# Doubled Strassen products: the order of wide and narrow matmuls in a decoder layer

## The chip, the cores and the metric

The kernel runs on one core of one Trainium2 chip. The engines are named as in the profile: PE (TensorE, matmuls), PEld (the weight loads of TensorE), DVE (VectorE), ACT (ScalarE), POOL (GpSimd) and SP (SyncE, which only issues DMAs here). The metric is the device time of one execution in microseconds; a kernel's time is the median of its runs.

## The reference, cut to what matters

One layer of a hybrid decoder on 512 tokens of width 2048, all in float32:

```python
h = rmsnorm(x, attn_norm_g[i])
proj = h @ w_in[i]                    # 2048 -> u, v, q, k, v_att (5 x 1024), g_a, g_b (2 x 2048)
y_a = chunked_spatial_gating(u, v_sgu, w_s[i], b_s[i])     # after gelu and a norm of v
y_b = stick_breaking_attention(q, k, v_att)                # 8 heads of 128, blocks of 128
merged = sigmoid(g_a) * (y_a @ w_up_a[i]) + sigmoid(g_b) * (y_b @ w_up_b[i])
x = x + merged @ w_o[i]
hid = rmsnorm(x, ffn_norm_g[i]) @ w_ffn_in[i]              # 2048 -> 2 x 5632
x = x + (silu(hid[..., :5632]) * hid[..., 5632:]) @ w_ffn_out[i]
x = x + sigmoid(rmsnorm(x, ple_norm_g[i]) @ w_ple_gate[i]) * (p[i] @ w_ple[i])
```

## The kernel before, in words

Everything is kept transposed: features on the 128 partitions, the 512 tokens along the free axis. A number is split into a high part, which the fast matmul format holds exactly, and a low rest (`split_into`, L266 and L267; for weights `split`, L331 on DVE and L334 on ACT). A product of two split numbers takes three matmuls: high by high, high by low, low by high (`mm3`, L271 to L273).

A matrix product is cut into *pairs*: a `Pair` computes one block of 256 output features for all 512 tokens. Its contraction over 2048 features has eight units of 256, of kind S (one step of Strassen: the 2 by 2 blocks need seven products of 128 x 128 weights with 256 tokens instead of eight) or P (plain). Two neighbouring units of one kind share a load of weights, so a pair of eight S units consists of four *calls* of `Pair.add`, each with two units (`n = 2`), that is with 7 x 2 products.

In two stages the pairs are *doubled* (`doubled=7` in the FFN input, 43 pairs; `doubled=5` in the input projection, 33 pairs). A doubled product owns a PSUM bank of 512 columns, and the three matmuls become two, both at L629 of the kernel before:

- a **wide** one ("both"): the high half of the weights against high and low half of the tokens side by side, 512 columns;
- a **narrow** one ("low"): the low half of the weights against the high half of the tokens, 256 columns, added to the first half of the bank.

With `doubled=5` the last two products of a call go through `mm3` with 256 columns and share the bank "y". Products 1 to 6 of `doubled=7` (0 to 5 in the code) take the six banks of the pool `psm`; the seventh takes one of the two banks of the pool `psa`, whose tiles the profile calls "small".

In a pair's first call the matmuls of a product clear its bank (`start`); in its last call (`stop`) each finished product is taken out of PSUM and mixed into the four output blocks by `mix_doubled` (ACT copies at L685, DVE additions at L688), step by step with `next(mix)`. Only when the last reader of a bank is done may the next pair write it.

The order on PE is that of the program, except where the tile framework's planner, which runs over the traced program with a model of the times, finds the next matmul not ready and takes a later one. On ACT and DVE the splits of weights and the mixing are chained in the order in which they were written (`in_turn`). Weights arrive ahead of their use: `prepare_early` at the head of a call and `prepare_late` after its third product advance the weights of the next two calls by a step (load on SP, an accumulating load on POOL at L338, sums on DVE at L350, splits); there are three slots of split weights (`whi`, `wlo`), and a call gives its slot back at its end. After the products listed in `TICKS` (the fourth and the seventh) `tick()` places pieces of other work: attention, gating, the forms of the next inputs.

In the kernel before, the two units of one doubled product follow each other as wide, narrow, narrow, wide.

Of the kernel before, what the change touches and what calls it, by code (L numbers as in the profile page):

```python
# [65 lines left out]
def hybrid_layer(  # L66
# [18 lines left out]
    nc = tc.nc  # L85
# [9 lines left out]
    def nm(s):  # L95
        return f"{s}_{next(names)}"
# [75 lines left out]

    def wide():
        return tmp.tile([P, 1024], F32, tag="out", name=nm("out"))
# [14 lines left out]
    def mark(instruction):  # L189
        newest[instruction.ins.engine] = instruction.ins.name  # L190
# [4 lines left out]
    def traced():  # L195
        return nc.cur_bb.bb.instructions

    def tick():

        clock[0] += 1  # L200
        last, units = traced()[-1], dict(newest)
        for f in list(builds)[:AHEAD]:
            if not f.there and f.ready() and fits([(wholes, 1024, "old"), (wholes, 1024, "low")]):
                f.fetch()
                break
        if builds and builds[0].ready() and builds[0].arrived() and fits(builds[0].sizes):
            builds.popleft().step()
        while waiting and waiting[0][0] <= clock[0]:
            heapq.heappop(waiting)[2]()
        for i in reversed(traced()):  # L210
            if i is last:
                break
            if i.engine in units:
                tc.add_manual_dep(
                    i, units[i.engine],
                    mybir.DependencyInfo(mybir.DependencyClass.NoSync,
                                         mybir.DependencyReason.DATA),
                    reason="in its place among the units")
# [50 lines left out]
    def mm3(ps, sh, sl, mh, ml, start, stop, halved=False):  # L269
        for s in (slice(0, 256), slice(256, T)) if halved else (slice(None),):  # L270
            nc.tensor.matmul(ps[:, s], sh, mh[:, s], start=start, stop=False)  # L271
        nc.tensor.matmul(ps, sh, ml, start=False, stop=False)  # L272
        return nc.tensor.matmul(ps, sl, mh, start=False, stop=stop)  # L273
# [109 lines left out]
    def prepare_early():  # L383

        if prepared:
            prepared[0].to(4)
        if len(prepared) > 1 and (slots or prepared[1].step > 1):
            prepared[1].to(3)

    def prepare_late():  # L390

        if len(prepared) > 1 and prepared[1].step > 1:
            prepared[1].to(4)
        for w in list(prepared)[2:]:
            w.to(1)
        ahead(8)

    def ahead(n):
        while planned and landings and len(prepared) < n:
            prepared.append(Weights(*planned.popleft()))  # L400
# [76 lines left out]
    def load(src, n=1024, how="old"):  # L477
        b = take(n, how)
        nc.sync.dma_start(out=b.f(0, 1024), in_=src)
        return b  # L480
# [91 lines left out]
    class Pair:  # L572
# [21 lines left out]
        def add(self, kind, ws, xs, prepare=True):  # L594
            n = len(ws)
            start = self.left[kind] == self.n[kind]
            self.left[kind] -= n
            stop = self.left[kind] == 0
            if prepare:
                prepare_early()  # L600
            if kind == "P":
                for u, ((wh, wl), (xh, xl)) in enumerate(zip(ws, xs)):
                    for ps, bs in zip(self.ends(), ((2, 3), (0, 1))):
                        for k, b in enumerate(bs):
                            first = start and u + k == 0

                            mark(mm3(ps, wh[:, b], wl[:, b], xh[k], xl[k],
                                     first and not self.both, stop and u == n - 1 and k == 1,
                                     first and self.both and b < 2))
                    if prepare and u == 0:  # L610
                        prepare_late()
                    tick()
                return

            if stop:
                o = self.home()
                self.o = wide() if o is None else o
                mix = (self.mix_doubled if self.doubled else self.mix)(self.o)
            for i, ((name, h), (w, x)) in enumerate(zip(HALVES, PRODUCTS)):
                for u, ((wh, wl), t) in enumerate(zip(ws, xs)):  # L620
                    first, last = start and u == 0, stop and u == n - 1
                    if i < self.doubled:
                        ps = self.at(i)
                        both = ps, wh[:, w], t[:, x].rearrange("p s c -> p (s c)")
                        low = ps[:, :256], wl[:, w], t[:, x, 0]

                        work = (low, both) if u else (both, low)
                        for k, (out, l, r) in enumerate(work):
                            m = nc.tensor.matmul(out, l, r, start=first and k == 0,  # L629
                                                 stop=last and k == 1)  # L630
                        mark(m)
                    else:


                        ps = self.at(name)[:, 256 * h : 256 * h + 256]
                        ends = not (self.both and name in "yz") and (h == 1 or name == "z")
                        mark(mm3(ps, wh[:, w], wl[:, w], t[:, x, 0], t[:, x, 1],
                                 first and h == 0, last and ends))
                if stop:
                    next(mix)  # L640
                if i == 2:
                    prepare_late()
                if i in TICKS[n]:
                    tick()

        def mix(self, o):

# [27 lines left out]
        def mix_doubled(self, o):  # L675
# [4 lines left out]
            c11, c12, c21, c22 = (b[:, i] for i in range(4))  # L680
            s5 = tmp.tile([P, 256], F32, tag="p5", name=nm("p5"), bufs=1)
            add, sub = ALU.add, ALU.subtract

            def copy(out, x, scale=1.0):
# [10 lines left out]
            yield  # L695
            copy(c22, p7[0])
            tt(c12, c12, c11, add)
            tt(c22, c22, p7[1], add)
            yield
            copy(s5, p5[0])  # L700
# [219 lines left out]
    def x_form(k):  # L920
        def steps(form):
            while len(x_raw) < min(k + 2, KU):
                load_x()
            form.blocks = (parts.take(2 * PLACE, "place"),)
            w = take(1024, "old")
            gained(w.f(), x_raw[k].f(), g_attn, k)
            norm1.add(x_raw[k])
            give(x_raw[k])
            yield
            yield from plain_first(form, w)  # L930
            return form.operand()

        return Form("S", steps, [], always)

    xs = [x_form(k) for k in range(KU)]
# [221 lines left out]
    order = []  # L1157
# [68 lines left out]
    for n, ((w, i), pr) in enumerate(zip(order, made())):  # L1226
# [24 lines left out]
        else:  # L1251
            d = tc.dram_tile([P, 1024], F32, name=nm("gsp"))
# [6 lines left out]
    part, merged = {}, {}  # L1259
# [30 lines left out]
    there = set()  # L1290
# [7 lines left out]
    for j in range(KU):  # L1298
# [9 lines left out]
        h = raw.popleft()  # L1308
# [37 lines left out]
    at = 0  # L1346
    for c, kinds in enumerate(PASSES):
        units, first = hs[at : at + len(kinds)], at
# [3 lines left out]
        for j in range(KU):  # L1352
# [6 lines left out]
            h = before.f()  # L1359
# [128 lines left out]
```

## Time and profile before

| what | value |
|---|---|
| time, three runs | 2701.99, 2707.65, 2710.27 us; median 2707.65 us |
| profiled execution | span 2701.9 us, which is the run of 2701.99 us to a tenth |
| PE busy | 2668.1 us (99%), 15875 matmuls |
| DVE busy | 2147.0 us (79%) |
| ACT busy | 1367.3 us (51%) |
| POOL busy | 459.0 us (17%) |
| DMA | 529.40 MB, mean 196 GB/s |

The windows of the trace that the text speaks of are, in us from the start: 0 to 87 the start of the input projection, 87 to 830 the rest of it with attention and gating beside it, 830 to 1204 the up and output projections, 1204 to 2047 the FFN input, 2047 to 2702 the FFN output and the last gate.

Matmuls are pipelined: the durations that the profile gives for them overlap, so a row of the timeline is read by its start, and the time that a matmul costs is the distance to the next start. Where neighbouring instructions of one line are merged, "x2" stands behind the row and the second start falls in between. PE's busy share hides short waits for the same reason.

### The profile page before, as it was taken

How to read it: one execution, taken by the hardware profiler on the slowest of the kernel's cores; microseconds unless marked ns; L12 is line 12 of the kernel's file. 1: busy time of each engine (PE TensorE's matmuls, PEld its weight loads, DVE VectorE, ACT ScalarE, POOL GpSimd, SP SyncE). 2: the span in 40 equal slices, each digit the busy share in tenths (PEclk: the TensorE clock that was granted, in tenths of full speed). 3: DMA queues.
4: the chain of work that ended last, by engine and by line, in shares of the span. 5: the costliest groups of instructions: out<-in, count | busy, mean ns of one | idle time of the engine just before them, and what ended most of it. 6: DMA issues, size and time to landing. Idle time of an engine off the chain costs nothing.

```text
span 2701.9 us, 43167 instructions
## 1 busy us (share of the span) xinstructions
PE 2668.1 (99%) x15875; PEld 2354.6 (87%) x15875; DVE 2147.0 (79%) x3621; ACT 1367.3 (51%) x2143; POOL 459.0 (17%) x543
## 2 busy tenths in 40 slices
PE   8999999999999999999999999999999999999999
PEld 6888888989998889988888888888888999988898
DVE  7687878787887566688988888888889667688776
ACT  7656565655554343374444444444445344453543
POOL 0232323232220000001111111111111111110110
PEclk9999999999999999999999999999999999999999
DMA  7677777777776467678888888888887668688784
GB/s 224 156 185 175 181 173 186 170 187 197 177 186 197 140 173 200 173 219 211 212 212 202 200 203 205 201 198 210 195 210 206 181 167 262 184 249 236 218 243 133
DMA packets 303268, 529.40 MB, mean 196 GB/s; under 512 B 25680, under 2 KB 162896, under 8 KB 303056
## 3 DMA queue, kind: packets, MB, share of 16 engines
q1 hardware_dynamic: 242304, 426.22, 49.9%
q0 software_dynamic: 60752, 100.43, 23.8%
q8 instruction: 124, 2.03, 0.3%
q14 instruction: 88, 0.72, 0.1%
HBM read 479.36 MB, written 47.19 MB: 195 GB/s over the span
## 4 chain that ended last, share of the span: by engine, by line
PE 88%; DVE 5%; DMA 2%; ACT 2%; issue 1%; POOL 1%; SPq 0%; DVEq 0%; ACTq 0%; POOLq 0%
PE ps L629 39%; PE ps L272 14%; PE ps L273 14%; PE ps L271 14%; PE small L629 4%; DVE wlo L331 2%; DVE out L688 1%; PE small L1084 1%; PE small L959 1%; ACT whi L334 1%; DMA wholes<-w_in 0%; DMA wholes<-w_first 0%; DVE wholes L350 0%; PE small L1034 0%; DVE parts L267 0%
## 5 line engine op out<-in xcount | busy, mean ns | idle before, releaser
L334 ACT ACTIVATE whi<-wholes 128x512 fp32r<-128x512 f32 (+4 forms) x950 | 857.6, 917 | 838.3 <-DVE wholes L350 261.9
L629 PE MATMUL ps<-parts,whi 128*128 128x512 f32 x3384 | 1134.8, 398 | 0.3 <-DVE p L688 0.3
L331 DVE TENSOR_TENSOR wlo<-wholes,whi 128x512 fp32r<-128x512 f32 (+4 forms) x950 | 962.4, 1046 | 101.0 <-ACT whi L334 100.5
L271 PE MATMUL ps<-parts,whi 128*128 128x256 f32 (+1 forms) x2675 | 855.1, 323 | 15.7 <-ACT parts L266 9.7
L272 PE MATMUL ps<-parts,whi 128*128 128x256 f32 (+1 forms) x2640 | 857.0, 325 | 1.0 <-DVE parts L267 0.8
L273 PE MATMUL ps<-parts,wlo 128*128 128x256 f32 (+1 forms) x2640 | 855.9, 325 | 0.9 <-DVE wlo L331 0.9
L629 PEld LDWEIGHTS ps<-parts,wlo 128*128 128x128 f32 x3384 | 635.8, 188 | 142.6 <-issue 1.0
L629 PE MATMUL ps<-parts,wlo 128*128 128x256 f32 x3384 | 671.1, 279 | 0.0
L271 PEld LDWEIGHTS ps<-parts,whi 128*128 128x128 f32 x2675 | 508.8, 190 | 60.7 <-ACT parts L266 10.8
L629 PEld LDWEIGHTS ps<-parts,whi 128*128 128x128 f32 x3384 | 545.3, 189 | 5.0 <-issue 1.0
L272 PEld LDWEIGHTS ps<-parts,whi 128*128 128x128 f32 x2640 | 502.7, 191 | 47.2 <-DVE parts L267 2.8
L273 PEld LDWEIGHTS ps<-parts,wlo 128*128 128x128 f32 x2640 | 502.7, 191 | 41.2 <-DVE wlo L331 2.8
L350 DVE TENSOR_TENSOR wholes<-wholes 128x256 f32<-128x256 f32 (+1 forms) x794 | 326.8, 412 | 21.8 <-DMA wholes<-w_ffn_out 4.0
L338 POOL DMA_DIRECT2D wholes<-w_ffn_in x172 | 149.7, 871 | 693.0 <-DVE wholes L350 238.8
L688 DVE TENSOR_TENSOR out<-out,ps 128x256 f32<-128x256 f32 x388 | 160.3, 415 | 131.7 <-ACT out L685 131.5
L338 POOL DMA_DIRECT2D wholes<-w_in x132 | 118.0, 895 | 486.1 <-DVE wholes L350 145.7
L655 DVE TENSOR_TENSOR out<-out 128x256 f32<-128x256 f32 x144 | 60.9, 423 | 114.7 <-ACT out L652 112.2
L629 PE MATMUL small<-parts,whi 128*128 128x512 f32 x344 | 136.5, 397 | 0.0
L267 DVE TENSOR_TENSOR parts<-wholes,parts 128x1024 fp32r<-128x1024 f32 (+4 forms) x131 | 123.7, 950 | 14.9 <-ACT parts L266 14.5
L266 ACT ACTIVATE parts<-wholes 128x1024 fp32r<-128x1024 f32 (+4 forms) x131 | 105.8, 834 | 42.0 <-DVE wholes L497 20.0
L338 POOL DMA_DIRECT2D wholes<-w_ffn_out x56 | 56.9, 1020 | 403.4 <-DMA wholes<-w_ffn_out 139.6
L1328 ACT ACTIVATE out<-out 128x512 f32<-128x512 f32 x44 | 27.8, 633 | 157.9 <-DVE out L1327 157.9
(121 smaller groups left out, 1655.0 us busy)
## 6 DMA issues: line engine op xcount, KB each, us to landing
wholes<-w_ffn_in SPq DMA_DIRECT2D x172, 384.0 KB, 5.6
wholes<-w_in SPq DMA_DIRECT2D x132, 384.0 KB, 4.9
wholes<-w_ffn_in SPq DMA_DIRECT2D x172, 256.0 KB, 4.8
wholes<-w_ffn_in POOLq DMA_DIRECT2D x172, 256.0 KB, 5.4
wholes<-w_in SPq DMA_DIRECT2D x132, 256.0 KB, 4.2
wholes<-w_in POOLq DMA_DIRECT2D x132, 256.0 KB, 5.0
wholes<-x SPq DMA_DIRECT2D x33, 512.0 KB, 5.5
wholes<-w_ffn_out SPq DMA_DIRECT2D x31, 512.0 KB, 4.5
```

The lines of the kernel that those rows point to most:

```text
L266: return (nc.scalar.activation(hi, src, AF.Copy), nc.vector.tensor_tensor(out=lo, in0=src, in1=hi.bitcast(F32), op=ALU.subtract))
L267: nc.vector.tensor_tensor(out=lo, in0=src, in1=hi.bitcast(F32), op=ALU.subtract))
L271: nc.tensor.matmul(ps[:, s], sh, mh[:, s], start=start, stop=False)
L272: nc.tensor.matmul(ps, sh, ml, start=False, stop=False)
L273: return nc.tensor.matmul(ps, sl, mh, start=False, stop=stop)
L331: in_turn(nc.vector.tensor_tensor(out=self.lo[:, blocks], in0=r, in1=h.bitcast(F32), op=ALU.subtract))
L334: in_turn(nc.scalar.activation(h, r, AF.Copy))
L338: nc.gpsimd.dma_start(out=raw[:, 3:5], in_=self.src[:, 1:3], accum_op=ALU.add)
L350: in_turn(nc.vector.tensor_tensor(out=o, in0=x, in1=y, op=ALU.add))
L629: m = nc.tensor.matmul(out, l, r, start=first and k == 0, stop=last and k == 1)
L655: in_turn(nc.vector.tensor_tensor(out=out, in0=x, in1=y, op=op))
L688: in_turn(nc.vector.tensor_tensor(out=out, in0=x, in1=y, op=op))
```

## The change

The loop over products and units in `Pair.add` becomes a list of jobs, each a product, a part of it ("both", "low" or, where not doubled, "single") and a unit. A new method `order` gives the sequence:

- in a pair's **first** call the products go by twos: both wide parts of the two products (four matmuls with the two units), then the four narrow ones;
- in its **last** call likewise by twos, with the narrow ones first;
- in the **second** call all narrow ones of all doubled products, then all wide ones; in the **third** all wide ones, then all narrow ones. Undoubled products stand at the head of the second call and at the end of the others.

At the edges between calls the widths meet: first call narrow to second call narrow, wide to wide, narrow to narrow, and a pair ends and the next begins wide (with `doubled=7`). The steps of the mixing, `prepare_late` and the ticks hang on places in the list: in a last call on the last job of their product, elsewhere on the same share of the list as before. Only the wide matmul of the first unit clears a bank. For pairs that are not doubled the sequence stays what it was.

```diff
-            for i, ((name, h), (w, x)) in enumerate(zip(HALVES, PRODUCTS)):
-                for u, ((wh, wl), t) in enumerate(zip(ws, xs)):
-                    first, last = start and u == 0, stop and u == n - 1
-                    if i < self.doubled:
-                        ps = self.at(i)
-                        both = ps, wh[:, w], t[:, x].rearrange("p s c -> p (s c)")
-                        low = ps[:, :256], wl[:, w], t[:, x, 0]
-
-                        work = (low, both) if u else (both, low)
-                        for k, (out, l, r) in enumerate(work):
-                            m = nc.tensor.matmul(out, l, r, start=first and k == 0,
-                                                 stop=last and k == 1)
-                        mark(m)
...
-                if stop:
-                    next(mix)
-                if i == 2:
-                    prepare_late()
-                if i in TICKS[n]:
-                    tick()
+            def product(i, part, u):
+                name, h = HALVES[i]
+                w, x = PRODUCTS[i]
+                (wh, wl), t = ws[u], xs[u]
+                first, last = start and u == 0, stop and u == n - 1
+                if part == "both":
+                    return nc.tensor.matmul(self.at(i), wh[:, w],
+                                            t[:, x].rearrange("p s c -> p (s c)"),
+                                            start=first, stop=last)
+                if part == "low":
+                    return nc.tensor.matmul(self.at(i)[:, :256], wl[:, w], t[:, x, 0],
+                                            start=False, stop=False)
...
+            jobs = [(i, part, u) for i, part in self.order(start, stop) for u in range(n)]
+            at = [max(k for k, job in enumerate(jobs) if job[0] == i) if stop
+                  else -(-(i + 1) * len(jobs) // len(PRODUCTS)) - 1 for i in range(len(PRODUCTS))]
+            for k, job in enumerate(jobs):
+                mark(product(*job))
+                for i in (i for i, there in enumerate(at) if there == k):
+                    if stop:
+                        next(mix)
+                    if i == 2:
+                        prepare_late()
+                    if i in TICKS[n]:
+                        tick()
+
+        def order(self, start, stop):
+            d = self.doubled
+            single = [(i, "single") for i in range(d, len(PRODUCTS))]
+
+            def turn(low, products):
+                return [(i, part) for part in (("both", "low"), ("low", "both"))[low]
+                        for i in products]
+
+            if start or stop:
+                return [x for a in range(0, d, 2)
+                        for x in turn(stop, range(a, min(a + 2, d)))] + single
+            if self.left["S"] // 2 % 2:
+                return turn(False, range(d)) + single
+            return single + turn(True, range(d))
```

More of the change, by code (lines that the diff above doesn't have):

```diff
@@ L618, in add @@
                 mix = (self.mix_doubled if self.doubled else self.mix)(self.o)
-            for i, ((name, h), (w, x)) in enumerate(zip(HALVES, PRODUCTS)):
-                for u, ((wh, wl), t) in enumerate(zip(ws, xs)):
-                    first, last = start and u == 0, stop and u == n - 1
-                    if i < self.doubled:
-                        ps = self.at(i)
-                        both = ps, wh[:, w], t[:, x].rearrange("p s c -> p (s c)")
-                        low = ps[:, :256], wl[:, w], t[:, x, 0]
-                        work = (low, both) if u else (both, low)
-                        for k, (out, l, r) in enumerate(work):
-                            m = nc.tensor.matmul(out, l, r, start=first and k == 0,
-                                                 stop=last and k == 1)
-                        mark(m)
[L632 to L638, printed above, removed]
-                if stop:
-                    next(mix)
-                if i == 2:
-                    prepare_late()
-                if i in TICKS[n]:
-                    tick()
@@ new lines, in product @@
+            def product(i, part, u):
[10 more added lines that the diff above has]
+                                            start=False, stop=False)
+                ps = self.at(name)[:, 256 * h : 256 * h + 256]
+                ends = not (self.both and name in "yz") and (h == 1 or name == "z")
+                return mm3(ps, wh[:, w], wl[:, w], t[:, x, 0], t[:, x, 1],
+                           first and h == 0, last and ends)
```

## The prediction

> **What bounds the kernel now.** I read the page's busy shares first, then the chain that ended last, then the groups by line.
>
> ```profile
> span 2701.9 us, 43167 instructions
> ...
> PE 2668.1 (99%) x15875; PEld 2354.6 (87%) x15875; DVE 2147.0 (79%) x3621; ACT 1367.3 (51%) x2143; POOL 459.0 (17%) x543
> ...
> PE 88%; DVE 5%; DMA 2%; ACT 2%; issue 1%; POOL 1%; SPq 0%; DVEq 0%; ACTq 0%; POOLq 0%
> ...
> L629 PE MATMUL ps<-parts,whi 128*128 128x512 f32 x3384 | 1134.8, 398 | 0.3 <-DVE p L688 0.3
> L629 PE MATMUL small<-parts,whi 128*128 128x512 f32 x344 | 136.5, 397 | 0.0
> ```
>
> TensorE (PE) is the bound: 99% busy and 88% of the chain. L629 is the line that the change rewrites. It holds 3384 + 344 = 3728 wide matmuls (512 columns) and as many narrow ones (256), 1864 groups of two wide and two narrow: 43 pairs x 28 groups in the FFN input, 33 x 20 in the input projection. The mean of 398 ns is no price, since matmuls overlap. The price is the distance from one start to the next, so everything below is read from the timeline.
>
> The windows of the FFN input stage and, under it, the narrow matmuls of the seventh product (tile small):
>
> ```profile
> 1204.00:2047.00 843.00, 843.00 (x4830) 734.96 (x4829) 747.82 (x1340) 411.75 (x573) 147.06 (x169) 1.00 0.82 203
> ```
> ```profile
> L629 PE MATMUL small<-parts,wlo x344: 274/277/285, 1211.0 to 2046.7; 128*128 128x256 f32 x172
> ```
>
> The first row gives the busy time of PE, weight loads, DVE, ACT and POOL, then the granted clock, the DMA share and GB/s. PE has no idle time in this stage, at clock 1.00; DVE is the next engine, 747.82 of 843 us. Two such matmuls belong to a call, so there are 172 calls, and (2046.7 - 1211.0) / 171 = 4.887 us is the time of one call of seven products: 0.698 us per group.
>
> **The price of a width, of a run and of a switch.** First the present order, around the edge between two pairs (x2 means two in a row; the start is the first one's):
>
> ```profile
> 1539.37 0.39 PE L629 MATMUL ps<-parts,whi 128*128 128x512 f32 x1
> 1539.60 0.40 PE L629 MATMUL ps<-parts,wlo 128*128 128x256 f32 x2
> 1539.84 0.63 PE L629 MATMUL ps<-parts,whi 128*128 128x512 f32 x2
> 1540.30 0.39 PE L629 MATMUL ps<-parts,wlo 128*128 128x256 f32 x2
> 1540.53 0.62 PE L629 MATMUL ps<-parts,whi 128*128 128x512 f32 x2
> ...
> 1542.62 0.40 PE L629 MATMUL ps<-parts,whi 128*128 128x512 f32 x1
> 1542.86 0.40 PE L629 MATMUL small<-parts,whi 128*128 128x512 f32 x1
> 1543.09 0.28 PE L629 MATMUL small<-parts,wlo 128*128 128x256 f32 x1
> 1543.21 0.39 PE L629 MATMUL ps<-parts,whi 128*128 128x512 f32 x1
> ```
>
> Two wide ones take 0.46 (1539.84 to 1540.30), two narrow ones 0.23. Long runs of one width exist already, in the undoubled products (L271 to L273): a wide run, and the start of a narrow one.
>
> ```profile
> 1199.74 0.39 PE L272 MATMUL ps<-parts,whi 128*128 128x512 f32 x1
> ...
> 1204.05 0.39 PE L273 MATMUL ps<-parts,wlo 128*128 128x512 f32 x1
> ```
> ```profile
> 1042.12 0.28 PE L271 MATMUL ps<-parts,whi 128*128 128x256 f32 x1
> ...
> 1042.59 0.28 PE L272 MATMUL ps<-parts,whi 128*128 128x256 f32 x1
> ```
>
> The wide run has 19 steps in 4.31 us, 0.2268 each, against 0.233 in the present order. The narrow run is 84 matmuls long (two calls of 42) and ends where the next fence begins: (1052.19 - 1042.12) / 84 = 0.1199 each, against 0.115 in the present order. So a long run makes the wide ones cheaper and the narrow ones dearer. A group would cost 2 x (0.2268 + 0.1199) = 0.693 against 0.698. What a switch costs is seen where that narrow run ends:
>
> ```profile
> 1052.19 0.40 PE L271 MATMUL ps<-parts,whi 128*128 128x512 f32 x1
> 1052.42 0.40 PE L272 MATMUL ps<-parts,whi 128*128 128x512 f32 x1
> 1052.66 0.39 PE L273 MATMUL ps<-parts,wlo 128*128 128x512 f32 x1
> 1052.89 0.40 PE L271 MATMUL ps<-parts,whi 128*128 128x512 f32 x1
> 1053.12 0.39 PE L272 MATMUL ps<-parts,whi 128*128 128x512 f32 x1
> 1053.35 0.39 PE L273 MATMUL ps<-parts,wlo 128*128 128x512 f32 x1
> 1053.58 0.40 PE L271 MATMUL ps<-parts,whi 128*128 128x256 f32 x2
> 1053.81 0.40 PE L272 MATMUL ps<-parts,whi 128*128 128x512 f32 x1
> ```
>
> The first two wide matmuls after a switch take 0.47 (0.016 over the steady price), the first four 0.93 (0.023 over), all six 1.39 (0.029 over). The two narrow ones behind them take 0.23, 0.01 under; the four of 1042.12 to 1042.59 take 0.47, also 0.01 under. One round of wide and narrow therefore costs about 0.02 over the steady price if it is long, 0.013 if it is four and four.
>
> **The change part by part.** No matmul, copy, addition or DMA is added or removed; the order on PE changes.
>
> (a) *FFN input, per pair.* With calls 1 and 4 by twos and calls 2 and 3 whole, neighbouring runs join: wide runs of 6, 4, 4, 2, 28, 4, 4, 4 and narrow ones of 4, 4, 4, 16, 18, 4, 4, 2. Their excess: 2 x 0.029 + 5 x 0.023 + 0.016 = 0.189, less 8 x 0.01 = 0.109 us. Now it is 4 x 4.887 - 28 x 0.693 = 0.144 by the rounded price, 0.133 by 28 x 2 x 0.3467. I take the latter: 0.024 us less, x 43 pairs = -1.0 us.
>
> (b) *Input projection, per pair* (five doubled products): wide runs of 4, 4, 2, 20, 4, 4, 2, excess 4 x 0.023 + 2 x 0.016 + 0.029 - 7 x 0.01 = 0.083, against 20 x 0.0047 = 0.095 now (0.133 / 28 a group): x 33 = -0.4 us. The undoubled products keep their width and price. Bounds for (a) and (b) together: all excess gone, 1864 x 0.0047 = -8.8 us; or no discount for the narrow ones behind a run of four, 5 x 43 + 4 x 33 = 347 times 0.01, some +3.5 us.
>
> (c) *PSUM, the new wait.* In a pair's last call the third product now ends after 4 narrow, 4 wide, 4 narrow and 2 wide matmuls (0.47 + 0.93 + 0.47 + 0.47 = 2.34 us) instead of three groups (2.09), 0.25 later. Behind its additions DVE's queue holds the splits of the next weights, and behind those the rest of the mixing, which gives the banks back:
>
> ```profile
> 1537.64 2.08 DVE L331 TENSOR_TENSOR wlo<-wholes,whi 128x1280 fp32r<-128x1280 f32 x2
> ...
> 1541.36 0.41 DVE L688 TENSOR_TENSOR out<-out,ps 128x256 f32<-128x256 f32 x1
> ...
> 1542.36 0.41 DVE L688 TENSOR_TENSOR out<-out,ps 128x256 f32<-128x256 f32 x1
> ```
>
> The fifth product's bank is free at 1541.77, the sixth's at 1542.77. In the next pair the row 1542.62 is the fifth product's last wide matmul; its first lies a wide and two narrow ones earlier (0.23 + 0.23), at 1542.16. The sixth starts at 1543.21. The slacks are 0.39 and 0.44. With the chain 0.25 later the fifth still has 0.14. The sixth is now wanted 0.47 after the fifth, at 1542.63, and would be free at 1543.02: a wait of 0.39 if PE takes it in the written order. It need not: the rows 1542.86 and 1543.09 show that the planner already puts the seventh product ahead of the sixth here. The fifth's two narrow (0.23) and the seventh's two wide ones (0.47) cover the wait. Bounds: 0 and 43 x 0.39 = +17 us. I take 0.03 a pair, +1.3 us, nearest to the row in which the gap was filled.
>
> (d) *Weights.* Whole calls that begin with the narrow ones want all low halves of a call within 1.7 us of its start. The splits above are written for the call after next and end at 1537.64 + 2.08 = 1539.72, while that call starts one call after 1539.37, at 1544.26: 4.5 us in hand, price 0. The high halves of a slot are given back at most 0.25 later (call 2) and 1.5 earlier (call 3); ACT, 411.75 of 843 us busy, covers it.
>
> (e) *Preparation.* In a last call the loads issued after the third product (two on SP, one accumulating on POOL) move 0.25 us later, in other calls not at all or by 0.3. They are issued more than a call ahead; price 0. If that cover went, 0.25 x 76 pairs = 19 us would be the end. In the projection PE waits for the attention alone:
>
> ```profile
> PE small L1069 <- DVE parts L1062: 3.6, 4, 0.9
> ```
>
> Such waits move with the order, by at most their own size, up or down: 0, bounds -3 and +3.
>
> **Sum:** -1.0 - 0.4 + 1.3 = 0. The profiled execution took 2701.99 us about its span of 2701.9, the lowest of three; their median is 2707.65. A forecast of no change is 2707.5 as a median.
>
> **Rivals.**
> 1. *Runs give what they are meant to:* wide at 0.2268 and narrow still at 0.115, a group at 0.684: 1864 x -0.0136 = -25, 2682 us. For it: both prices occur in the trace. Against it: they never occur in one run; the 84 narrow ones cost 0.1199. Chance 0.08. A milder one: the excess goes altogether (-8.8) and the attention's waits shrink (-3): 2696 us, 0.16.
> 2. *The sixth bank (slower):* the planner believes the bank free and PE, which then stands still, waits 0.39 us in 43 pairs: +17, 2724 us. It decides from 0.2 us a pair on (+8.6). For it: DVE is busy 747.82 of 843 us. Against it: the filled gap above. Chance 0.14.
> 3. *Narrow runs dear, wide ones not cheaper (slower):* runs of four wide cost 0.93, 0.2325 each, hardly under today's 0.233; if the long ones in whole calls did so too, narrow at 0.1199 gives 1864 x 2 x 0.0049 = +18, 2726 us. Against it: 0.2268 in the wide run. Chance 0.10.
>
> The Trainium skill, "TensorE: Matmul & The Clock Gate", section "LDWEIGHTS (loading the stationary operand)", puts a load of 128 columns at P / 1.2, 107 ns. By that rule a narrow matmul streams no longer than the load of its successor takes, and only a wide neighbour hides it, which is the mechanism of rival 3 and speaks against rival 1. The trace's 0.1199 in the narrow run against 0.115 among wide ones agrees in sign.
>
> **How the numbers follow.** A measurement of this kernel tells about 0.3% (8 us: the three runs span 2701.99 to 2710.27) from no change. No change within that: 0.52. Faster: 0.08 + 0.16 = 0.24. Slower: 0.14 + 0.10 = 0.24. The predicted time is that of the likeliest case, 2707.5; its own range is 2700 to 2715. The range for 8 in 10 reaches to most of the milder faster case and into rivals 2 and 3: 2688 to 2722.
>
> **What would show it.** Right: in the FFN stage wide runs of 28 at 0.227 and narrow runs at 0.120 after a first pair at 0.23; a pair's four calls still near 19.5 us; PE without waits there. Rival 1: narrow runs at 0.115. Rival 2: a repeated wait of L688 before a pair's fifth or sixth product. Wrong would also be any new order in which PE waits for the low halves (L331) at the head of a call.

## The result and the profile after

The changed kernel takes 2713.77 us (median of 7 runs, 2712.9 to 2715.82), the kernel before in the same session 2707.19 us (7 runs, 2698.29 to 2710.82). The ratio is 1.0033, 95% interval 1.0021 to 1.0045: slower by about 0.3%, where no change was forecast. The profiled execution is a run of 2715.56 us. The profile before is of a run of 2701.99 us, so the two profiles lie 13.6 us apart and the medians 6.6: what the traces show below is the difference of these two executions, about twice that of the medians.

The page of the changed kernel, in the lines that answer to those of before. The wide matmuls are now L628, the narrow ones L632:

```profile
span 2713.9 us, 43165 instructions
...
PE 2668.7 (98%) x15875; PEld 2364.6 (87%) x15875; DVE 2150.8 (79%) x3621; ACT 1364.7 (50%) x2143; POOL 455.5 (17%) x543
...
PE 81%; DVE 9%; ACT 4%; DMA 3%; issue 2%; POOL 1%; SPq 0%; DVEq 0%; ACTq 0%; POOLq 0%
...
L628 PE MATMUL ps<-parts,whi 128*128 128x512 f32 x3384 | 888.0, 394 | 1.6 <-DVE p L713 0.8
```

The busy sums of the engines are what they were. (L628 shows 888.0 us where L629 had 1134.8, at the same count and nearly the same mean: wide neighbours overlap now, and a busy time counts an overlap once.) The chain is not: PE falls from 88% to 81% of it, DVE rises from 5% to 9%, ACT from 2% to 4%. PE waits for other engines more than before. Where, the windows say. They run from the first to the last doubled matmul of the input projection and of the FFN input; the columns are length, busy time of PE, weight loads, DVE, ACT and POOL, granted clock, DMA share and GB/s. First the kernel before, then the changed one:

```profile
87.10:824.00 736.90, 727.09 (x4629) 647.60 (x4628) 591.18 (x1053) 441.71 (x907) 209.49 (x264) 1.00 0.74 182
1204.30:2046.80 842.50, 842.50 (x4828) 734.63 (x4827) 747.32 (x1340) 411.25 (x573) 147.06 (x169) 1.00 0.82 203
```
```profile
87.50:837.50 750.00, 730.89 (x4630) 653.03 (x4629) 592.46 (x1053) 438.89 (x906) 205.79 (x264) 0.99 0.72 178
1218.40:2060.40 842.00, 841.99 (x4829) 740.98 (x4827) 750.80 (x1339) 411.15 (x573) 147.26 (x169) 1.00 0.82 204
```

The FFN input, 43 of the 76 changed pairs, is 0.5 us shorter in these rounded windows (0.6 from start to start) and PE has no idle time in it. The input projection is 13.1 us longer, and PE's idle time there grows from 9.8 us (736.90 - 727.09) to 19.1. So the loss between the two profiles lies in the stage that runs beside attention and gating. PE's waits in that stage, of the changed kernel (us in total, times, longest; `parts` and `wholes` are the kernel's two pools of work tiles):

```profile
PE small L984 <- ACT wholes L1006: 5.3, 1, 5.3
PE small L1109 <- POOL wholes L1100: 4.6, 8, 0.7
PE small L1094 <- DVE parts L1087: 3.9, 4, 1.3
PE small L1166 <- ACT wholes L1006: 2.9, 2, 2.6
```

and of the kernel before, where the third of these was 3.6 us and the others were:

```profile
PE small L959 <- ACT wholes L981: 2.5, 1, 2.5
PE small L1084 <- POOL wholes L1075: 2.2, 4, 0.6
...
PE small L1141 <- ACT wholes L981: 0.5, 1, 0.5
```

All are steps of the attention and of the norms (transposes L984, running sums of the attention's scores with a triangular matrix L1094, weighted values L1109, the gating's mixing L1166). None is a doubled matmul. These four waits grow from 8.8 to 16.7 us. An interruption can also be measured from the start of the plain matmul ahead of such a step to the start of the second plain one behind it, less the steady prices of two (0.2267 us for 512 columns, 0.120 for 256). All interruptions together cost 86.3 us before and 98.6 after: 12.3 of the 13 us. The excess over these prices at all other plain matmuls goes from 4.4 to 5.0.

How a wait grows is seen in single rows. Gating's mixing, kernel before (start, duration, engine, line; in brackets the idle time before and its releaser):

```profile
648.60 0.17 DVE L1132 TENSOR_SCALAR ms<-ms 128x4 f32<-128x4 f32 x1
...
649.44 0.86 POOL L338 DMA_DIRECT2D wholes<-w_in  x1 [1.29 <-DVE ms L1132]
650.00 1.61 POOL L858 TENSOR_TENSOR rr<-ms,expo 128x4 f32<-128x4 f32 x1
651.64 1.14 ACT L981 ACTIVATE wholes<-small,rr 128x128 f32<-128x128 f32 x4 [2.56 <-POOL rr L858]
652.06 1.26 PE L1141 MATMUL small<-wholes 128*128 128x128 f32 x8 [0.54 <-ACT wholes L981]
```

and the changed kernel:

```profile
659.24 0.16 DVE L1157 TENSOR_SCALAR ms<-ms 128x4 f32<-128x4 f32 x1
...
661.03 0.86 POOL L338 DMA_DIRECT2D wholes<-w_in  x1 [3.88 <-DMA wholes<-w_in]
661.59 1.37 POOL L883 TENSOR_TENSOR rr<-ms,expo 128x4 f32<-128x4 f32 x1
663.00 1.14 ACT L1006 ACTIVATE wholes<-small,rr 128x128 f32<-128x128 f32 x4 [4.63 <-POOL rr L883]
663.41 0.98 PE L1166 MATMUL small<-wholes 128*128 128x128 f32 x4 [2.64 <-ACT wholes L1006]
```

The power on POOL has its input at 659.40, but in POOL's queue an accumulating load stands ahead of it, and that one waits until 661.03 for an earlier load to land. In the kernel before the load ahead of the power went at 649.44, 0.7 us after the input. The traces show POOL's instructions in one order, the load and then the power, in both kernels, so the power, the products on ACT and PE's matmuls all wait for a weight load. What differs in this place is not POOL's order but when the earlier load landed: by the trace's semaphores 5.7 us after its issue, and 3.6 in the kernel before. This one wait does not tell the kernels apart either: it is 1.3 us in ffn_only and 2.4 in after_old_queues (both below), which lose nothing. The weighted values show a wait behind a weight split on ACT, kernel before and after:

```profile
289.92 1.28 ACT L334 ACTIVATE whi<-wholes 128x1280 fp32r<-128x1280 f32 x1
291.41 0.62 ACT L1074 ACTIVATE wholes<-wholes 128x512 f32<-128x512 f32 x1
291.93 0.29 ACT L1058 ACTIVATE parts<-wholes 128x128 fp32r<-128x128 f32 x1
292.44 1.13 PE L1084 MATMUL small<-wholes 128*128 128x512 f32 x2
```
```profile
296.59 0.31 ACT L1083 ACTIVATE parts<-wholes 128x128 fp32r<-128x128 f32 x1 [0.94 <-POOL wholes L1072]
...
297.11 1.26 ACT L334 ACTIVATE whi<-wholes 128x1280 fp32r<-128x1280 f32 x1
298.27 0.62 ACT L1099 ACTIVATE wholes<-wholes 128x512 f32<-128x512 f32 x1
299.30 1.13 PE L1109 MATMUL small<-wholes 128*128 128x512 f32 x2 [0.53 <-POOL wholes L1100]
```

Before, the weight split is over 0.2 us ahead of the exponential (289.92 + 1.28 = 291.20). Afterwards the exponential begins only when the split is over, and PE waits 0.53. Here the order on ACT has changed: the copy to `parts` (L1058, now L1083) stood behind the exponential and now stands ahead of split and exponential, where ACT stood idle for 0.94 us until POOL was done.

Laid side by side engine by engine, the two traces have different instructions at 62 places on DVE, 120 on ACT and 11 on POOL (rows of one line with the same operands count as equal), although the diff touches only matmuls. The planner that orders the program had rearranged the other engines too.

### The profile page after: what moved, and what is told of

It is laid out like the page before. It is cut to its first block, busy times and chain, and to the rows that moved or that the text cites. A ratio compares the mean times of both kernels' runs of the same rounds, so it can differ in the third digit from the quotient of the medians.

```text
span 2713.9 us, 43165 instructions
## 1 busy us (share of the span) xinstructions
PE 2668.7 (98%) x15875; PEld 2364.6 (87%) x15875; DVE 2150.8 (79%) x3621; ACT 1364.7 (50%) x2143; POOL 455.5 (17%) x543
## 4 chain that ended last, share of the span: by engine, by line
PE 81%; DVE 9%; ACT 4%; DMA 3%; issue 2%; POOL 1%; SPq 0%; DVEq 0%; ACTq 0%; POOLq 0%
PE ps L628 23%; PE ps L272 14%; PE ps L273 13%; PE ps L271 13%; PE ps L632 12%; PE small L628 3%; DVE wlo L331 3%; DVE out L713 2%; PE small L632 1%; ACT whi L334 1%; DVE wholes L350 1%; DMA wholes<-w_in 1%; PE small L1109 1%; DVE parts L267 1%; PE small L984 0%
## 5 line engine op out<-in xcount | busy, mean ns | idle before, releaser
L628 PE MATMUL ps<-parts,whi 128*128 128x512 f32 x3384 | 888.0, 394 | 1.6 <-DVE p L713 0.8
L628 PEld LDWEIGHTS ps<-parts,whi 128*128 128x128 f32 x3384 | 603.6, 189 | 103.6 <-DVE p L713 1.7
L271 PEld LDWEIGHTS ps<-parts,whi 128*128 128x128 f32 x2675 | 509.0, 190 | 63.2 <-ACT parts L266 10.5
L272 PEld LDWEIGHTS ps<-parts,whi 128*128 128x128 f32 x2640 | 502.9, 191 | 42.7 <-DVE parts L267 3.1
L273 PEld LDWEIGHTS ps<-parts,wlo 128*128 128x128 f32 x2640 | 502.7, 191 | 41.2 <-DVE wlo L331 3.3
L632 PEld LDWEIGHTS ps<-parts,wlo 128*128 128x128 f32 x3384 | 486.1, 190 | 44.9 <-issue 1.9
L632 PE MATMUL ps<-parts,wlo 128*128 128x256 f32 x3384 | 517.4, 283 | 0.0
L710 ACT ACTIVATE out<-ps 128x256 f32<-128x256 f32 x207 | 76.9, 383 | 110.8 <-PE ps L628 106.9
```

Of the source, the lines that this page charges most:

```text
L628: return nc.tensor.matmul(self.at(i), wh[:, w], t[:, x].rearrange("p s c -> p (s c)"), start=first, stop=last)
L632: return nc.tensor.matmul(self.at(i)[:, :256], wl[:, w], t[:, x, 0], start=False, stop=False)
```

## Experiments

Each row: median, ratio to the kernel before on the same chip with its 95% interval, and the lengths of the two changed stages in the profiled execution (first to last doubled matmul). The rows stem from several chips, so the ratios are to be compared and not the medians.

| kernel | us | ratio | projection | FFN input |
|---|---|---|---|---|
| before | 2707.19 | 1 | 736.7 | 842.6 |
| changed | 2713.77 | 1.0033 [1.0021, 1.0045] | 749.7 | 842.0 |
| ffn_only | 2703.55 | 0.9993 [0.9983, 1.0003] | 737.7 | 841.8 |
| proj_only | 2717.68 | 1.0039 [1.0026, 1.0053] | 746.8 | 842.5 |
| twos_only | 2705.06 | 0.9992 [0.9982, 1.0002] | 739.9 | 844.6 |
| whole_only | 2708.36 | 1.0005 [0.9996, 1.0014] | 741.7 | 840.9 |
| proj_places_time | 2716.37 | 1.0043 [1.0029, 1.0057] | 745.4 | 842.5 |
| woven_places_share | 2707.43 | 1.0010 [1.0001, 1.0019] | 738.9 | 842.6 |
| bare_woven | 2620.69 | 0.9686 [0.9673, 0.9699] | 651.3 | 842.5 |
| bare_runs | 2617.82 | 0.9676 [0.9661, 0.9690] | 648.4 | 842.5 |
| runs_old_queues | 2704.55 | 1.0000 [0.9992, 1.0009] | 739.3 | 842.5 |
| woven_new_queues | 2713.40 | 1.0026 [1.0016, 1.0037] | 751.4 | 842.5 |
| after_old_queues | 2706.43 | 0.9997 [0.9989, 1.0006] | 738.2 | 841.8 |
| runs_old_act | 2718.52 | 1.0044 [1.0031, 1.0056] | 748.9 | 842.5 |
| runs_old_pool | 2713.75 | 1.0028 [1.0017, 1.0038] | 745.5 | 842.5 |
| runs_old_act_dve | 2713.68 | 1.0032 [1.0020, 1.0044] | 744.0 | 842.5 |

### Which stage, and which part of the order

Four kernels take a part of the change: one stage alone (ffn_only, proj_only), or in both stages one kind of call alone, the other kind left as it was ("woven": wide, narrow, narrow, wide per product).

```diff
+            d, edge = self.doubled, start or stop
+            woven = d != 7        # ffn_only;   d != 5: proj_only
+                                  # not edge: twos_only;   edge: whole_only
+            jobs = ([(i, part, u) for i in range(len(PRODUCTS)) for u in range(n)
+                     for part in ((("both", "low"), ("low", "both"))[u > 0] if i < d
+                                  else ("single",))]
+                    if woven else
+                    [(i, part, u) for i, part in self.order(start, stop) for u in range(n)])
```

> The new order in the FFN input alone (doubled by seven), the woven order of before in the input projection. Theory A (the loss comes from the input projection, where the attention's steps meet the matmuls at other points): as the kernel before within 0.1%, in the profile the FFN stage 0.6 us shorter than before and the projection as before, 737 us. Rival B (the runs themselves are dearer, in both stages in proportion to their groups, 1204 to 660): 4 us slower than before.

> The new order in the input projection alone, the FFN input as before. Theory A: the whole loss, 6 to 9 us slower than before as a median, and in the profile a projection of 748 to 750 us with 10 to 12 us more of it in the attention's interruptions. Rival B: 2 to 3 us slower.

> By twos in a pair's first and last call, in both doubled stages; the two middle calls keep the woven order of before. If the whole calls do the harm (C1: a whole call keeps the high halves of a slot until its end, and ACT stands at the next split): within 2 us of before. If the calls by twos do it (C2: the third product's mixing is later): as the changed kernel, 6 us slower.

> Whole calls in the middle, in both doubled stages; a pair's first and last call keep the woven order of before. C1 (whole calls do the harm): 5 to 8 us slower than before. C2 (calls by twos do): within 2 us of before, perhaps 1 to 2 us faster, since 28 wide ones in a row save some 0.04 us in each of 43 pairs.

The projection alone brings the whole loss (1.0039, some 11 us, more than the 6 to 9 expected; 10.5 us of it in the interruptions, 96.8 against 86.3), the FFN input alone none (0.9993). By kind of call the loss does not divide: neither calls by twos alone nor whole calls alone lose a measurable amount in time, though both lengthen the projection, by 3.2 and 5.0 us in the profiled executions. An explanation by one of the two kinds fell with that. The orders of the other engines do not divide either: against the trace of before, ffn_only and twos_only differ at 2 places on DVE, 2 on ACT and none on POOL, whole_only at 94, 136 and 13, proj_only at 60, 118 and 11. So whole_only has more changed places than proj_only and loses nothing that can be measured: their number alone does not tell the loss.

### Where in a call the other work stands

In the changed kernel the loads, splits and ticks of a call that is not the last hang on a share of the job list. In the first kernel here (projection alone in the new order) they hang on the time at which they stood before; in the second the old order of matmuls gets the new shares.

```diff
+            cost = {"both": 227, "low": 120, "single": 360}
+            done = np.cumsum([cost[part] for _, part, _ in jobs])
+            then = np.cumsum([n * (347 if i < d else 360) for i in range(len(PRODUCTS))])
+            by_time = [int(np.searchsorted(done, t)) for t in then]
```
```diff
-            woven = d != 5
+            woven = True
...
-            at = ([max(k for k, job in enumerate(jobs) if job[0] == i) for i in range(len(PRODUCTS))] if stop or woven
+            at = ([max(k for k, job in enumerate(jobs) if job[0] == i) for i in range(len(PRODUCTS))] if stop
```

> The runs in the input projection alone, as in proj_only, but in calls that do not end a pair the late preparation and the ticks hang on the job that PE reaches at the time at which the woven order reaches the third, fourth and seventh product, instead of on the same share of the list. If the moved places carry the loss (D1): within 2 us of before. If the order of the matmuls itself and the queues that the planner writes for it carry it (D2): as proj_only, 9 to 11 us slower than before.

> The woven order of before in both stages, but in calls that do not end a pair the late preparation and the ticks hang on the share of the list that the changed kernel uses, which in the input projection is 0.3 us earlier for the tick after the fourth product and one job later or earlier elsewhere. D1: 4 to 10 us slower than before. D2: within 2 us of before.

The places do not carry the loss. Put back, they leave it as it was (1.0043). Moved alone, they cost about 0.1% (0.01% to 0.19%), between the two forecasts; the trace of this kernel, too, has other orders on DVE, ACT and POOL (27, 49 and 8 places).

### Without the attention

Attention, the norms of queries and keys and the gating's mixing are left out in both kernels; their outputs are not computed. One has the old order, the other the new order in the projection.

```diff
-            beside(q_prep(o, i))
+            nc.sync.dma_start(out=y_spill[i], in_=o)
...
-            beside(attention(i, kT, rk, a_tile("v", 1024)), 6)
...
-            beside(v_prep(o, a_tile("v", 1024)))
...
-            beside(sgu_v(i, o))
```

> The woven order of before, with the attention, the norms of q and k and the mixing of the gating left out (q itself stands in for the attention's result, gelu alone for the gated half), so that PE does only the projection in that stage. Reference for bare_runs; by the interruptions of 86 us in the trace of before, 80 to 90 us less than before, about 2620 us.

> The runs in the input projection alone, with the same work left out as in bare_woven. Theory A (the loss is the attention's waits): within 2 us of bare_woven, the projection stage within 1 us. Rival B (the runs are dearer by themselves, or the weights come late): 6 to 10 us above bare_woven.

Without that work the new order loses nothing: the projection takes 648.4 us against 651.3, 2.9 less (the times' intervals overlap), where at most 1 us was expected. The loss needs the steps that PE waits for.

### PE's order or the other engines' orders

Two things changed together: PE takes its matmuls in another order, and the planner wrote other orders for ACT, DVE and POOL. The first kernel has the new matmul order in the projection and the old orders elsewhere; the second the old matmul order and the orders that the planner wrote for proj_only. They are held by dependencies of order alone, up to the end of the projection:

```diff
+    by = {}
+    for i in traced():
+        by.setdefault(str(i.engine).split(".")[-1], []).append(i)
+    for e, moved in PINNED.items():
+        row = [by[e][k + by_] for k, by_ in enumerate(moved)]
+        for a, b in zip(row, row[1:]):
+            tc.add_manual_dep(
+                b, a.name,
+                mybir.DependencyInfo(mybir.DependencyClass.NoSync,
+                                     mybir.DependencyReason.DATA),
+                reason="in the order of the other kernel")
```

> TensorE takes the changed order of the doubled matmuls in the input projection alone (the FFN input keeps the old order), while ScalarE, VectorE and GpSimd are held, by order alone and without new data, to the sequence in which the kernel before issues its instructions up to the end of that projection. Theory E1, the sequences that the planner rewrote on ScalarE, VectorE and GpSimd carry the loss: the time falls back to that of the kernel before, ratio 1.000 within 0.001, some 2705 to 2709 us, and TensorE's waits on the wholes and parts of ScalarE and GpSimd return to 3.6, 2.5 and 2.2 us per their rows of before. Theory E2, TensorE's own sequence carries it (attention steps stand at other matmuls than before and so come too early for their inputs): the time stays where the projection alone put it, ratio 1.003 to 1.005, some 2715 to 2718 us. In between, 2709 to 2715 us, both have a share.

> The mirror of the run beside it: TensorE keeps the order of matmuls of the kernel before, while ScalarE, VectorE and GpSimd are held to the sequence that the planner wrote for them when the projection alone was changed. Theory E1: the sequences bring the loss with them, ratio 1.003 to 1.005, some 2714 to 2719 us, and TensorE's waits on the wholes of ScalarE and GpSimd show 4 to 5 us each as with the changed projection. Theory E2: no loss, ratio 1.000 within 0.001, some 2705 to 2709 us.

This decides between the two. With the old orders the new matmul order costs nothing (1.0000); with the new orders the old matmul order loses 0.26%. The traces show the orders as intended: DVE, ACT and POOL of the first kernel nowhere differ from the kernel before, those of the second nowhere from proj_only. PE's order is not held. Of its 15875 matmuls the first kernel has 98 at other places than proj_only, the second 165 at other places than the kernel before: the planner moved steps of the attention by a few matmuls. How much of the difference goes through these moves is open. PE's waits in the projection, first with the new matmuls and old queues, then with the old matmuls and new queues (lines lie 13 further down than in the changed kernel: L997 is the transpose, L1107 the running sums, L1122 the weighted values, L1179 the mixing):

```profile
PE small L1122 <- POOL wholes L1113: 3.8, 4, 1.3
PE small L1107 <- DVE parts L1100: 2.9, 4, 0.8
PE small L997 <- ACT wholes L1019: 2.1, 1, 2.1
PE small L1179 <- ACT wholes L1019: 1.6, 1, 1.6
```
```profile
PE small L1107 <- DVE parts L1100: 5.2, 4, 1.9
PE small L1122 <- POOL wholes L1113: 4.6, 8, 0.6
PE small L997 <- ACT wholes L1019: 4.2, 1, 4.2
PE ps L635 <- DVE out L726: 2.6, 1, 2.6
PE small L1179 <- ACT wholes L1019: 2.3, 1, 2.3
```

10.4 against 18.9 us; the kernel before has 8.8 (3.6 + 2.5 + 2.2 + 0.5). In the second sum 2.6 us are waits for the additions that free a bank (L635). The forecast that each of these waits would return to its size of before did not hold: the values' wait is 3.8 us and not 2.2, the mixing's 1.6 and not 0.5; it is the sum that falls. The second profile is of the longest of that kernel's 8 runs (2720.12), so its 18.9 is rather high.

### The whole change with the old queues, and the engines one by one

after_old_queues is the whole change with all three orders held as above. The others have the new order in the projection and hold one or two engines; the planner orders the rest.

```diff
+PINNED = {"Activation": ..., "DVE": ..., "Pool": ...}   # after_old_queues
+PINNED = {"Activation": ...}                            # runs_old_act
+PINNED = {"Pool": ...}                                  # runs_old_pool
+PINNED = {"Activation": ..., "DVE": ...}                # runs_old_act_dve
```

> The whole change, both stages, with ScalarE, VectorE and GpSimd held to the kernel before's sequence up to the end of the input projection, as in the run with the projection alone. If the sequences are the whole loss, the projection gives back its 13 us and the FFN input keeps its 0.6 us: ratio 0.9985 to 1.0005, some 2701 to 2706 us beside about 2705 for the kernel before. If the loss needs something else of the whole change, it stays at 1.002 or more, 2711 us or more.

> The changed order in the input projection alone, and only ScalarE is held to its sequence of before; GpSimd and VectorE are left to the planner. If ScalarE's queue carries the loss (weight splits ahead of the attention's exponentials and of the normalization's products), ratio 0.999 to 1.0015, some 2703 to 2709 us. If GpSimd's queue carries it (products and masks behind accumulating loads), it stays near 1.004, 2713 to 2718 us.

> The mirror: only GpSimd is held to its sequence of before, 16 lines of it against the changed projection; TensorE and VectorE keep the changed projection's sequence and ScalarE all but 4 lines of it. If GpSimd's queue carries the loss, ratio 0.999 to 1.0015, some 2703 to 2709 us. If ScalarE's does, it stays near 1.004, 2713 to 2718 us. Both short of the full recovery, 1.0015 to 1.003 in each, would mean that they share it.

> The changed order in the input projection alone, with ScalarE and VectorE held to their sequences of before and GpSimd left to the planner, which puts 18 lines of GpSimd's queue (accumulating loads against the masks, products and powers) elsewhere than before. With ScalarE alone held the attention's waits were gone and 6.0 us of TensorE's waits on VectorE's evictions had come instead. If those came from VectorE's own sequence, they go: ratio 0.999 to 1.0015, some 2703 to 2709 us. If they came from GpSimd's loads standing ahead of products that VectorE waits for (18.8 us of VectorE's waits on GpSimd there, 5.5 us in the kernel before), they stay, and with them a ratio of 1.003 to 1.005, 2713 to 2718 us.

The whole change without the new queues is neutral: 0.9997. It does not beat the kernel before by anything that can be measured, and no other kernel here that computes the whole layer does.

No engine alone carries the loss, and both forecasts of a single one fell. With ACT held, the interruptions by the attention drop from 96.8 us (proj_only) to 87.7, nearly the 86.3 of before, and yet the time stays at 1.0044, because other waits have come: the excess at the other plain matmuls is 15.2 us instead of 4.0. In runs_old_act, PE's new wait and the wait of DVE behind it:

```profile
PE ps L633 <- DVE out L724: 6.0, 4, 2.5
```
```profile
DVE wholes L1107 <- POOL wholes L1090: 18.8, 12, 4.7
```

The kernel before has for the second

```profile
DVE wholes L1071 <- POOL wholes L1054: 5.5, 8, 1.0
```

POOL, whose order is now the planner's (other instructions than before at 20 places), clears the rows of the attention's sums late. DVE waits for them in its own queue, and the additions that free PE's banks stand in that queue too. With DVE held as well, POOL free (15 places), PE's wait on these additions falls to 2.7 us and DVE's on POOL to 10.4, so DVE's own order may have had a share; but the ratio is still 1.0032, and the excess at the other plain matmuls 8.2 us instead of 4.1 with all three held. That rest comes with POOL's order, though PE's steps moved with it (338 places against proj_only). Holding POOL alone leaves the interruptions at 95.4; this trace has PE's and DVE's order of proj_only and differs from it at 11 places on POOL and 3 on ACT. So POOL's old order is needed beside those of ACT and DVE, and it is not enough alone. Whether ACT's or DVE's must be held with it was not separated, and which lines would do was not tried.

## Why the prediction was wrong

**(a) FFN input, -1.0 us: right.** The prices read from existing runs held. The changed kernel around a pair's second and third call:

```profile
1557.82 0.40 PE L632 MATMUL ps<-parts,wlo 128*128 128x256 f32 x2
...
1559.97 2.91 PE L628 MATMUL ps<-parts,whi 128*128 128x512 f32 x12
...
1566.35 1.59 PE L632 MATMUL ps<-parts,wlo 128*128 128x256 f32 x12
...
1568.50 1.09 PE L628 MATMUL ps<-parts,whi 128*128 128x512 f32 x4
1569.43 0.63 PE L632 MATMUL ps<-parts,wlo 128*128 128x256 f32 x4
1569.90 1.09 PE L628 MATMUL ps<-parts,whi 128*128 128x512 f32 x4
```

28 wide ones take 6.38 us (1559.97 to 1566.35), 0.228 each with the first ones dearer; 18 narrow ones 2.15 (1566.35 to 1568.50), 0.1194 each; four wide after a switch 0.93, four narrow 0.47. The stage is 0.6 us shorter, where the sum with step (c) said +0.3. The two halves of it measure -1.6 (whole_only) and +2.0 us (twos_only): by the prediction's prices, 43 x (two calls of twos with an excess of 3 x 0.023 + 0.016 - 4 x 0.01 = 0.045 each, less two woven calls of 0.033) is +1.0, and 43 x (0.029 - 2 x 0.01 for two joined whole calls, one wide and two narrow runs, less 0.066) is -2.5. So the signs come out, the sizes only roughly. The Trainium skill's rule of P / 1.2, 107 ns for a load of 128 columns ("TensorE: Matmul & The Clock Gate", "LDWEIGHTS (loading the stationary operand)") agrees only in so far as the narrow ones, at 0.119 in the new runs too, do not come under it; the rows of the weight loads (187 to 192 ns each) overlap and give no price.

**(b) Input projection, -0.4 us: right in sign.** Without the attention the stage gains 2.9 us; the term was too small, within the bound of -8.8.

**(c) The sixth bank, +1.3 us: not there.** PE has no recorded wait at all in the FFN input. The planner puts the seventh product ahead of the sixth in the pair's first call, as it did before (wide ones at 1576.41 and 1576.87). Rival 2 is out, as are rivals 1 and 3: narrow runs stay at 0.119, and long wide runs are cheaper.

**(d) Weights: 0 in the FFN input, right.** PE waits for no low half there.

**(e) Preparation and attention waits, "0, bounds -3 and +3": the step that failed.** It measured +12.3 us in the projection, between two executions whose times differ by about twice the medians' 6.6 us. Two assumptions stood behind it. The first, that such waits move "by at most their own size", is refuted by rows: the mixing's wait went from 0.5 to 2.9 us, the transposes' from 2.5 to 5.3. The bound should have been how long the producer can stand in its queue behind work that is not urgent. The second was the sentence "the order on PE changes", without a word that the planner orders ACT, DVE and POOL from the same model of times. The runs with held queues show that the rewritten queues carry the loss, with the moves of PE's own steps that came with them. The prediction shows only one row of these waits (3.6 us, on DVE, now 3.9); those on ACT and POOL are the ones that grew.

The chance of slower, 0.24, lay on PSUM and on run prices, mechanisms that did not occur. The value 2707.5 is 6.3 us under the result. That the range 2688 to 2722 holds it is luck: its upper part stood for rivals 2 and 3.

## What to carry to other kernels

Where a planner orders the program, a change of one engine's order can change every engine's: compare the written queues of all engines before costing the change at nothing. An in-order engine that both feeds the bottleneck with small urgent steps and prepares far-off weights can hand the bottleneck the wait of a load; a "wait that only moves" is bounded by what can stand ahead of its producer, not by the wait seen today. When holding one queue moves the loss elsewhere and holding all of them removes it, the queues belong together and are best kept together.

## What was not expected of the hardware

A gap on PE can cost more than its length. The changed kernel after the wait of 2.64 us at 663.41, as windows (the figure after POOL's is the granted clock) and as rows:

```profile
660.00:664.00 4.00, 1.36 (x11) 1.16 (x10) 0.23 (x1) 1.00 (x4) 1.93 (x2) 0.97 0.88 227
664.00:670.00 6.00, 6.00 (x30) 5.41 (x30) 3.04 (x6) 3.24 (x7) 1.21 (x2) 0.73 0.51 86
670.00:680.00 10.00, 10.00 (x78) 9.57 (x77) 9.90 (x17) 7.04 (x17) 2.10 (x2) 1.00 0.54 131
```
```profile
664.90 1.20 PE L632 MATMUL ps<-parts,wlo 128*128 128x256 f32 x4
665.90 1.68 PE L628 MATMUL ps<-parts,whi 128*128 128x512 f32 x4
667.42 0.64 PE L632 MATMUL ps<-parts,wlo 128*128 128x256 f32 x4
```

Four narrow matmuls take 1.00 us instead of 0.47 and four wide ones 1.52 instead of 0.93: 1.1 us on top of the wait, at a granted clock of 0.73. In the window from 296 to 302 us, around the wait of 0.53, the clock stays at 1.00. The Trainium skill ("TensorE: Matmul & The Clock Gate", "What's actually happening") halves the clock after an idle window of about 3.4 us. The slow stretch fits that length: 0.27 of 6 us lost makes 3.2 us at half speed. The gap ahead of it does not: 2.64 us were enough here. Nor does the length of the gap alone decide. In runs_old_act_dve a longer one at the same step left the clock at 1.00:

```profile
661.99 1.26 PE L1178 MATMUL small<-wholes 128*128 128x128 f32 x8 [2.92 <-ACT wholes L1018]
```
```profile
664.00:670.00 6.00, 6.00 (x40) 5.44 (x39) 5.22 (x11) 4.47 (x13) 0.83 (x1) 1.00 0.51 108
```

What else decides is not shown by these runs.

The FFN input, which runs beside no such work, took 842.5 or 842.6 us in the profiled execution of every kernel with its old order (eleven of them), while the times of whole runs of the kernel before spread over 12 us. A stage's length in one profile thus tells tenths of a microsecond where the time of a run does not.
